# Even mixer in steps: the other projections one by one between a group's chunks

## Chip, cores and metric

The kernel runs on one core of a Trainium2 chip. The metric is the device time in microseconds (us) of one execution, as the median of several runs. The profile is one further execution, recorded by the hardware profiler. Engines are named as in the profile: PE does matmuls (PEld loads its weights), DVE is the vector engine, ACT the scalar engine, POOL is GpSimd (which issues the gathers here), SP issues the plain DMAs.

## What is computed

A two-layer backbone over 512 latent tokens ("x") and 256 context tokens ("c"), width 1024. Layer 0 is the even mixer followed by a PEER expert layer, layer 1 the odd mixer followed by another. Only layer 0 processes the context's outputs. The even mixer, cut to what matters here:

```
def even_mixer(hx, hc, w_in, w_out, ...):
    def project(h, conv):
        sc_x, sc_b, sc_c, z, xbc, dt_raw = jnp.split(h @ w_in, [...], axis=-1)
        xbc = jax.nn.silu(conv(xbc, ssd_conv_w) + ssd_conv_b)
        xs, bm, cm = jnp.split(xbc, [SSD_WIDTH, ...], axis=-1)
    ...                      # 16 heads in 4 groups, each a chunked scan in both directions
    def finish(gates, ssd_in, y_ssd, conv):
        y_a = sc_b * conv(sc_c * sc_x, sc_conv_w)              # short convolution
        y_b = (y_ssd + d_skip[:, None] * ssd_in[0]).reshape(Bsz, T, SSD_WIDTH)
        y_b = group_rmsnorm(y_b * jax.nn.silu(z), ssd_norm_w, SSD_GROUPS)
        return jnp.concatenate([y_a, y_b], axis=-1) @ w_out
```

The PEER layer picks 128 experts per token; for each it takes the dot product of the token with one row of a table U, puts it through a gelu and a gate, and adds so much of one row of a table V.

## The kernel before

A framework records instructions in program order, and its scheduler then sets a fixed order for each engine: what was recorded first goes first where several are ready. Each engine runs its list in order. Tiles come from pools with a number of buffers (`bufs`); a tile that finds no free buffer waits for an older one's last reader.

`even_mixer` runs twice, first for the context (T = 256, two chunks of 128 tokens), later for x (T = 512, `nt` = 4 chunks). For each half `q` it runs `ssd(g)` for two groups, then `short_conv(q)`, then `out_proj`, which multiplies the eight 128-row tiles of `yT` (four from the short convolution, j = 3 and 2, taken first; four from the groups, j = 1 and 0) with `w_out` and adds to the stream (L467, L471, L472). Within `ssd(g, yT)`:

- Four projections `proj` (24 matmuls each, L227) with weights that `weight` loads as two raw tiles `wr` of 512 KB, splits on ACT into `wh` (L197) and on DVE into `wl` (L198). ACT and DVE take each projection through the convolution into `ch` (L503, L354, L356); one Silu over `ch` (L506).
- For each chunk: transposes to `tk` (L513, L514), scaled inputs `xe` (L518), a state contribution `con` (L520, L521). Then the recurrence over chunks on DVE (`sd` L533, `con` L536).
- For each chunk: products `cb` (L551), exponents from `srow` and `trow` (L559 to L563 on PE, L565 on ACT), a multiplication `E` on DVE (L566), four matmuls into `yp` (L572).
- The gate `z`, two more projections (L577). The norm: L581, L583 on DVE, a square on ACT (L584), a sum over partitions on PE (L587, two matmuls), ACT and DVE to L595, and L598 writes `yT`.

`short_conv(q)` has twelve projections in six weights of two tiles: `scx` (L480), the products `scx` (L484), `sca` (L486, L354, L356), `yT` (L491).

While x's even mixer runs, the context's expert dot products (`dots`) run on the engines that it leaves free: they are recorded behind it, so the scheduler fills them in. There are 256: POOL issues an indirect gather of 128 rows of U (`g`, 512 KB, L950) into one of `gbufs` buffers, and DVE takes the dot product with the tokens (L1055). After the mixer come the PEER layer of layer 0 for x (first L109, L126) and the context's sums over rows of V.

```
for q in range(2):
    yT = P.tile([128, 8, T], F32, name="yT", tag="yT", bufs=1)
    for g in (2 * q, 2 * q + 1):
        ssd(g, yT)
    short_conv(q, yT)
    out_proj((D + q * 512, q * 512), yT)
```

Of the kernel before, what the change touches and what calls it, by code (L numbers as in the profile page):

```python
# [39 lines left out]
def kslab(ap, c0, n):  # L40

    return ap[:, c0:c0 + n].rearrange("(k p) n -> p k n", p=128)
# [21 lines left out]
class Backbone:  # L64
# [368 lines left out]
    def even_mixer(self, hT, T, width, steps, states, res, P, stream):  # L433
# [38 lines left out]
                    nc.vector.tensor_add(res[c][:, ns], res[c][:, ns], t)  # L472

        def short_conv(quarter, yT):
            for b in range(2 * quarter, 2 * quarter + 2):
                wx = self.weight([kslab(W, b * 256, 256)], KT, 256)
                sx, acc = [], []
                for e in range(2):
                    sx.append(P.tile([128, T], F32, name="scx", tag="scx", bufs=2))
                    nc.scalar.activation(sx[e], proj(wx, e), AF.Copy)  # L480
                wc = self.weight([kslab(W, 2048 + b * 256, 256)], KT, 256)
                for e in range(2):
                    j = 2 * b + e
                    nc.vector.tensor_mul(sx[e], proj(wc, e), sx[e])  # L484
                    acc.append(P.tile([128, T], F32, name="sca", tag="sca", bufs=2))
                    nc.scalar.activation(acc[e], sx[e], AF.Copy, scale=self.sc_w[:, j, 1:2])  # L486
                    self.conv(acc[e], sx[e], self.sc_w[:, j], rows, width)
                wb = self.weight([kslab(W, 1024 + b * 256, 256)], KT, 256)
                for e in range(2):
                    j = 2 * b + e  # L490
                    self.hook(nc.vector.tensor_mul(yT[:, 4 + j % 4], proj(wb, e), acc[e]))  # L491

        def ssd(g, yT):
            h0 = 4 * g
            ch = (P0 if T > 256 and g % 2 == 0 else P).tile([128, 4, T], F32, name="ch", tag="ch", bufs=nb)
            for j, t in enumerate((2 * g, 2 * g + 1, 8 + g, 12 + g)):
                if j == 0:
                    w = self.weight([kslab(W, 4096 + g * 256, 256)], KT, 256)
                if j == 2:
                    w = self.weight([kslab(W, 5120 + g * 128, 128), kslab(W, 5632 + g * 128, 128)], KT, 256)  # L500
                ps = proj(w, j % 2)
                acc = ch[:, j, :]
                nc.scalar.activation(acc, ps, AF.Identity, bias=self.ssd_b[:, t:t + 1],  # L503
                                     scale=self.ssd_w[:, t, 1:2])
                self.conv(acc, ps, self.ssd_w[:, t], rows, width)
            nc.scalar.activation(ch, ch, AF.Silu)  # L506

            tk = P.tile([128, nt, 3, 128], F32, name="tk", tag="tk", bufs=nb)
            con = P.tile([128, nt, 2, 256], F32, name="con", tag="con", bufs=nb)
            for c in range(nt):  # L510
                ps = self.tr_tile()
                for j in range(3):
                    nc.tensor.transpose(ps[:, j], ch[:, j, c * 128:(c + 1) * 128], self.ident)  # L513
                nc.scalar.activation(tk[:, c], ps[:, :3], AF.Copy)  # L514
                xt = tk[:, c, 0:2].rearrange("p a (b q) -> p (a b) q", q=64)
                xe = P.tile([128, 2, 4, 64], F32, name="xe", tag="xe", bufs=nb)
                for d in range(2):
                    nc.vector.tensor_mul(xe[:, d], xt, tend[:, c, d, h0:h0 + 4, None].to_broadcast([128, 4, 64]))  # L518
                ps = self.mc_tile()
                nc.tensor.matmul(ps, tk[:, c, 2], xe.rearrange("p a h q -> p (a h q)"), start=True, stop=True)  # L520
                nc.scalar.activation(con[:, c].rearrange("p a n -> p (a n)"), ps, AF.Copy)  # L521

            st = {}
            for d in range(2):
# [18 lines left out]
            for d in range(2):  # L543
                k = d * 16 + h0
                self.load(srow[32 * d:32 * d + 12], parts[:, 32 + k:36 + k])
                self.load(trow[32 * d + 12:32 * d + 15], parts[:, k:k + 4])
            for c in range(nt):
                cs = slice(c * 128, (c + 1) * 128)
                B, C = ch[:, 2, cs], ch[:, 3, cs]
                ps = self.mc_tile()  # L550
                nc.tensor.matmul(ps[:, :128], B, C, start=True, stop=True)  # L551
                cb = P.tile([128, 128], F32, name="cb", tag="cb", bufs=2)
                nc.scalar.activation(cb, ps[:, :128], AF.Copy)
                terms = [(0, cb), (1, cb)] + [(d, C) for d in range(2) if st[c, d] is not None]
                for i, (d, by) in enumerate(terms):
                    kr = slice(32 * d, 32 * d + 15)
                    ps = self.mc_tile().rearrange("p (h t) -> p h t", h=4)
                    if i < 2:
                        nc.tensor.matmul(ps, srow[kr, cs], trow[kr, :, cs], start=True, stop=False)  # L559
                        nc.tensor.matmul(ps, self.identb, self.mneg[:, d, None, :].to_broadcast([128, 4, 128]),  # L560
                                         start=False, stop=True)
                    else:
                        nc.tensor.matmul(ps, self.sel[kr], trow[kr, :, cs], start=True, stop=True)  # L563
                    e = P.tile([128, 4, 128], F32, name="E", tag="E", bufs=4)
                    nc.scalar.activation(e, ps, AF.Exp)  # L565
                    ins = nc.vector.tensor_mul(e, e, by[:, None, :].to_broadcast([128, 4, 128]))  # L566
                    if i == 0:
                        self.hook(ins)
                    for h in range(4):
                        p, x = h // 2, h % 2 * 64  # L570
                        l = tk[:, c, p, x:x + 64] if i < 2 else st[c, d][:, h * 64:h * 64 + 64]
                        nc.tensor.matmul(yp[p][x:x + 64, cs], l, e[:, h], start=(i == 0),  # L572
                                         stop=(i == len(terms) - 1), skip_group_check=True)
# [8 lines left out]
                                               op0=OP.mult, op1=OP.add)  # L582
            nc.vector.tensor_mul(y, y, zs)  # L583
            nc.scalar.activation(sq, y, AF.Square)  # L584
            ps = self.mc_tile()
            for p in range(2):
                nc.tensor.matmul(ps[:, :T], self.ones, sq[:, p], start=(p == 0), stop=(p == 1))  # L587
            r, hv = sq[:, 0], sq[:, 1]
            t = P.tile([128, T], F32, name="nt", tag="scx", bufs=2)
            nc.scalar.activation(t, ps[:, :T], AF.Ln, scale=1.0 / 256, bias=self.epsc)  # L590
            nc.vector.tensor_scalar(hv, ps[:, :T], -0.5 / 256, -0.5 * EPS, op0=OP.mult, op1=OP.add)
            nc.scalar.activation(r, t, AF.Exp, scale=-0.5)
# [3 lines left out]
            for p in (1, 0):  # L596
                k = 2 * g + p
                nc.vector.scalar_tensor_tensor(yT[:, k % 4], y[:, p], self.snw[:, k:k + 1], r,  # L598
                                               op0=OP.mult, op1=OP.mult)

        for q in range(2):
            yT = P.tile([128, 8, T], F32, name="yT", tag="yT", bufs=1)
            for g in (2 * q, 2 * q + 1):
                ssd(g, yT)
            short_conv(q, yT)
            out_proj((D + q * 512, q * 512), yT)
        return fin

# [805 lines left out]
    def build(self):  # L1414
        tc, nc, io = self.tc, self.nc, self.io
        with ExitStack() as es:
# [104 lines left out]
            with tc.tile_pool(name="evenhx", bufs=1) as H, Pools(tc, "evenx") as P:  # L1521
# [7 lines left out]
                ch.__exit__(None, None, None)  # L1529
                ch = right("ch2")  # L1530
                hp = ch.__enter__()
                self.gpool, self.gbufs = hp, 6
                todo = [lambda t=t, h=h: self.dots(0, t, h) for t in ctoks for h in range(8)]
                todo.insert(8 + TU, lambda: self.turn(ctoks[0]))
                self.between([], 1)
# [64 lines left out]
```

## Time and profile before

| | us |
|---|---|
| median of 3 runs (4576.45 to 4588.05) | 4577.45 |
| the profiled execution, own time | 4589.98 |
| its span, first to last instruction | 4587.9 |
| PE busy | 4200.4 (92%) |
| DVE busy | 3416.2 (74%) |
| ACT busy | 1761.5 (38%) |
| POOL busy | 1507.3 (33%) |

The span of this execution is taken apart by stretches. The context's mixer lies at about 45 to 335 us, x's mixer at about 460 to 1142 us. An engine's busy share is read within one stretch, since the stretches have different limits; granted clock 1.00 stands for 2.4 GHz on TensorE and 0.50 for 1.2 GHz.

### The profile page before, as it was taken

To read this page: it belongs to the slowest core of one execution; us is meant where nothing else is said; L and a number is where in the kernel's file an instruction comes from. 1 tells how busy PE (TensorE), PEld (TensorE's weight loads), DVE (VectorE), ACT (ScalarE), POOL (GpSimd) and SP (SyncE) were. 2 spreads that over 40 slices of the span, in tenths; PEclk is the share of its full clock that TensorE was granted. 3 is DMA by queue.
4 is the path that set the end of the run, shared out by engine and by line. 5 is a ranking of instruction groups with operands and counts; after the bars stand their busy time and mean duration, and the time that the engine had idled before them with its cause. 6 is when DMAs were issued, how large, how long until landed. Compare 5 with 4: busy or idle time off the path is not lost. (4 is left out here: it accounts for less than half of the span.)

```text
span 4587.9 us, 60287 instructions
## 1 busy us (share of the span) xinstructions
PE 4200.4 (92%) x21452; PEld 3359.2 (73%) x21452; DVE 3416.2 (74%) x6826; ACT 1761.5 (38%) x3159; POOL 1507.3 (33%) x1114
## 2 busy tenths in 40 slices
PE   7989947969988789999999999998999999999998
PEld 4666625635534778888899988886857778888997
DVE  4556989973686979888788865666887548878887
ACT  4442312231224833333333335554447433333333
POOL 0002477640444355544455410000000005445452
PEclk9999958969999999999999999998999999999999
DMA  9538889952777899988898831221246758889886
GB/s 322 175 105 280 276 310 339 346 182 89 254 244 257 270 333 354 365 319 314 316 329 322 324 123 57 62 60 49 74 156 189 231 183 315 321 314 335 326 315 224
DMA packets 488766, 1119.51 MB, mean 244 GB/s; under 512 B 39793, under 2 KB 252337, under 8 KB 488465
## 3 DMA queue, kind: packets, MB, share of 16 engines
q1 hardware_dynamic: 334096, 553.55, 36.2%
q0 software_dynamic: 154368, 562.11, 33.9%
q8 instruction: 169, 2.77, 0.2%
q14 instruction: 133, 1.08, 0.1%
HBM read 1054.18 MB, written 60.82 MB: 243 GB/s over the span
## 5 line engine op out<-in xcount | busy, mean ns | idle before, releaser
L950 POOL DMA_INDIRECT g<-in_peer_u_dram,idx x256 | 373.7, 1460 | 934.3 <-DVE pre L1055 699.0
L198 DVE TENSOR_TENSOR wl<-wr,wh 128x1024 fp32r<-128x1024 f32 x404 | 493.3, 1222 | 197.2 <-ACT wh L197 195.2
L227 PE MATMUL yp<-hTh,wh 128*128 128x384 f32 x1808 | 610.9, 338 | 13.5 <-ACT wh L197 12.3
L227 PE MATMUL yp<-hTh,wl 128*128 128x384 f32 x1808 | 611.8, 338 | 6.0 <-DVE wl L198 5.9
L197 ACT ACTIVATE wh<-wr 128x1024 fp32r<-128x1024 f32 x404 | 426.6, 1057 | 489.8 <-DMA wr<-in_peer_uT_dram 223.7
L227 PE MATMUL yp<-hTl,wh 128*128 128x384 f32 x1808 | 608.4, 336 | 0.0
L950 POOL DMA_INDIRECT g<-in_peer_v_dram,idx x256 | 386.0, 1508 | 381.5 <-DVE y L1075 311.1
L950 POOL DMA_INDIRECT g<-in_peer_v_dram,idxc x256 | 340.0, 1328 | 397.5 <-DVE y L1075 162.5
L950 POOL DMA_INDIRECT g<-in_peer_u_dram,idxc x256 | 346.4, 1353 | 156.3 <-DVE prec L1055 62.5
L86 POOL TENSOR_TENSOR rs_y<-rs_v,mhalf 128x1 f32<-128x1 f32 (+2 forms) x29 | 22.7, 783 | 1089.4 <-DVE rs_v L85 1089.3
L227 PE MATMUL mm<-hTh,wh 128*128 128x512 f32 (+1 forms) x864 | 342.9, 398 | 21.7 <-ACT scx L480 11.4
L227 PEld LDWEIGHTS yp<-hTh,wh 128*128 128x128 f32 x1808 | 341.9, 189 | 27.9 <-ACT wh L197 14.1
L198 DVE TENSOR_TENSOR vl<-wr,vh 128x1024 fp32r<-128x1024 f32 x256 | 312.6, 1221 | 63.8 <-ACT vh L197 63.5
L227 PEld LDWEIGHTS yp<-hTh,wl 128*128 128x128 f32 x1808 | 341.2, 189 | 12.9 <-DVE wl L198 11.1
L1055 DVE CUSTOM_DVE_ANT_0 g<-g,h 128x1024 f32<-128x1024 f32 x256 | 305.9, 1221 | 60.1 <-DMA g<-in_peer_u_dram,idx 59.8
L227 PEld LDWEIGHTS yp<-hTl,wh 128*128 128x128 f32 x1808 | 341.6, 189 | 9.0
L227 PE MATMUL mm<-hTl,wh 128*128 128x512 f32 (+1 forms) x864 | 339.6, 393 | 0.2 <-DVE hTl L198 0.2
L1351 DVE TENSOR_TENSOR a<-a,gt 128x384 f32<-128x384 f32 x256 | 215.6, 846 | 164.3 <-ACT a L1239 81.3
L1075 DVE SCALAR_TENSOR_TENSOR y<-g,pre,y 128x1024 f32<-128x1024 f32 x254 | 325.4, 1281 | 16.2 <-DMA g<-in_peer_v_dram,idx 14.9
L227 PE MATMUL mm<-hTh,wl 128*128 128x512 f32 (+1 forms) x864 | 335.3, 391 | 0.6 <-DVE wl L198 0.6
L1055 DVE CUSTOM_DVE_ANT_0 g<-g,cx 128x1024 f32<-128x1024 f32 x256 | 308.0, 1220 | 31.8 <-DMA g<-in_peer_u_dram,idxc 30.6
L197 ACT ACTIVATE vh<-wr 128x1024 fp32r<-128x1024 f32 x256 | 270.1, 1055 | 155.9 <-PE mc L1373 74.6
(462 smaller groups left out, 9685.6 us busy)
## 6 DMA issues: line engine op xcount, KB each, us to landing
wr<-in_peer_v_dram SPq DMA_DIRECT2D x256, 512.0 KB
wr<-in_peer_uT_dram SPq DMA_DIRECT2D x226, 512.0 KB
gd<-stage SPq DMA_DIRECT2D x24, 2048.0 KB
gt<-gd SPq DMA_DIRECT2D x64, 768.0 KB
wr<-in_ev_w_in_dram SPq DMA_DIRECT2D x80, 512.0 KB
adaw<-in_ada_w_dram SPq DMA_DIRECT2D x48, 512.0 KB
adaw<-in_ada_w_dram POOLq DMA_DIRECT2D x48, 512.0 KB, 6.6
wr<-in_peer_wq_dram SPq DMA_DIRECT2D x40, 512.0 KB
```

Of the source, the lines that this page charges most:

```text
L86: nc.gpsimd.tensor_tensor(y, v, self.mhalf[:, :n], op=OP.pow)
L197: self.nc.scalar.activation(hi, src, AF.Copy)
L198: self.nc.vector.tensor_sub(lo, src, hi.bitcast(F32))
L227: mm(o, a, rhs(kk, i)[b], start=first and kk == 0 and n == 0, stop=last and kk == k - 1 and n == 2)
L950: self.nc.gpsimd.indirect_dma_start(out=g, out_offset=None, in_=table, in_offset=bass.IndirectOffsetOnAxis(ap=idx, axis=0), element_offset ...
L1055: self.nc.vector.tensor_tensor_reduce(g, g, t.h2, 1.0, 0.0, OP.mult, OP.add, s["pre"][:, k, h:h + 1])
L1075: nc.vector.scalar_tensor_tensor(t.y, g, a, t.y, op0=OP.mult, op1=OP.add)
L1351: self.last = nc.vector.tensor_mul(a, a, self.gt_[:, :, i % 4])
```

## The change

`ssd` is taken apart: the four projections with their convolution become a generator `ssd_in(g)`, which stops after each projection; `short_conv` becomes a generator that stops after each of its twelve. A group's `ssd(g, yT, other)` gets one of them as `other`: for the first group of a half that is the second group's projections, for the second group the short convolution. It takes one step of `other` in the norm, in both streams; for x (T > 256) also after the contributions of the second and the fourth chunk and ahead of the third chunk's products. What is left of a generator runs where all of it ran before. To make room: `xe` has 2 buffers in x (it had 1; 2 KB each per partition), the norm's `nt` a buffer of its own (it shared `scx`), and the gathers `g` have 5 buffers, not 6, while x's mixer runs.

```diff
@@ short_conv: becomes a generator
                     nc.scalar.activation(sx[e], proj(wx, e), AF.Copy)
+                    yield
...
                     self.conv(acc[e], sx[e], self.sc_w[:, j], rows, width)
+                    yield
...
                     self.hook(nc.vector.tensor_mul(yT[:, 4 + j % 4], proj(wb, e), acc[e]))
-
-        def ssd(g, yT):
-            h0 = 4 * g
-            ch = (P0 if T > 256 and g % 2 == 0 else P).tile([128, 4, T], F32, name="ch", tag="ch", bufs=nb)
+                    yield
+
+        chs = {}
+
+        def ssd_in(g):
+
+            chs[g] = ch = (P0 if T > 256 and g % 2 == 0 else P).tile([128, 4, T], F32, name="ch", tag="ch", bufs=nb)
...
                 self.conv(acc, ps, self.ssd_w[:, t], rows, width)
+                yield
+
+        def ssd(g, yT, other):
+
+            h0 = 4 * g
+            ch = chs.pop(g)
...
-                xe = P.tile([128, 2, 4, 64], F32, name="xe", tag="xe", bufs=nb)
+                xe = P.tile([128, 2, 4, 64], F32, name="xe", tag="xe", bufs=2)
...
                 nc.scalar.activation(con[:, c].rearrange("p a n -> p (a n)"), ps, AF.Copy)
+                if T > 256 and c % 2:
+                    next(other, None)
...
             for c in range(nt):
+                if T > 256 and c == 2:
+                    next(other, None)
...
             nc.scalar.activation(sq, y, AF.Square)
+            next(other, None)
...
-            t = P.tile([128, T], F32, name="nt", tag="scx", bufs=2)
+            t = P.tile([128, T], F32, name="nt", tag="nt", bufs=1)
...
+        def rest(steps):
+            for _ in steps:
+                pass
+
         for q in range(2):
             yT = P.tile([128, 8, T], F32, name="yT", tag="yT", bufs=1)
-            for g in (2 * q, 2 * q + 1):
-                ssd(g, yT)
-            short_conv(q, yT)
+            first, second, short = ssd_in(2 * q), ssd_in(2 * q + 1), short_conv(q, yT)
+            for steps, g, other in ((first, 2 * q, second), (second, 2 * q + 1, short)):
+                rest(steps)
+                ssd(g, yT, other)
+            rest(short)
             out_proj((D + q * 512, q * 512), yT)
...
-                self.gpool, self.gbufs = hp, 6
+                self.gpool, self.gbufs = hp, 5
```

Since recorded order is priority, the scheduler's lists move by more than these lines. Three places. The line numbers of the changed kernel are higher there: its L525, L532, L588, L604, L608, L615 and L1078 are L513, L520, L572, L587, L591, L598 and L1055 of before.

First, PE in x's mixer from the norm of group 0 on (L587, L604), into the chunks of group 1. Before:

```order
L587 MATMUL mc_4638<-yT_4191,ones_80 128x512 x2
L513 MATMUL mc_4792<-ident_69,ch_4650 128x128 x3
L520 MATMUL mc_4800<-xe_4797,tk_4790 128x512
L513 MATMUL mc_4803<-ident_69,ch_4650 128x128 x3
L520 MATMUL mc_4811<-xe_4808,tk_4790 128x512
L513 MATMUL mc_4814<-ident_69,ch_4650 128x128 x3
```

and of after, where `mm_5460` is a projection of the short convolution:

```order
L604 MATMUL mc_4777<-yT_4191,ones_80 128x512 x2
L525 MATMUL mc_4792<-ident_69,ch_4356 128x128 x3
L227 MATMUL mm_5460<-hTh_2921,wl_5451 128x512
L227 MATMUL mm_5460<-hTh_2921,wh_5450 128x512
L227 MATMUL mm_5460<-hTl_2922,wh_5450 128x512
```

Before, no projection stands between the norms of groups 0 and 1; now the first L532 has 51 projection matmuls ahead of it, and 214 (8.9 projections) stand between the two norms.

Second, DVE at the norm of the last group, group 3, in x (L583, L591 and so on). Before:

```order
L583 TENSOR_TENSOR ch_6087<-ch_6087,yT_5628 128x1024
L591 TENSOR_SCALAR yT_5628<-mc_6533 128x512
L484 TENSOR_TENSOR scx_6557<-mm_6623,scx_6557 128x512
L593 TENSOR_TENSOR nt_6536<-yT_5628 128x512
L594 TENSOR_TENSOR nt_6536<-nt_6536,yT_5628 128x512
L354 SCALAR_TENSOR_TENSOR sca_6649<-scx_6557,sc_w_3450,sca_6649 128x8x63
```

and of after, where the first two rows are the last of the 256 dot products:

```order
L1078 ISA g_7837,prec1_2845<-g_7837,cx1_112 128x1024
L1078 ISA prec1_2845 128x1
L608 TENSOR_SCALAR yT_5628<-mc_6671 128x512
L610 TENSOR_TENSOR nt_6674<-yT_5628 128x512
L1085 TENSOR_TENSOR prec1_2845<-prec1_2845,gatec1_2844 128x128
L611 TENSOR_TENSOR nt_6674<-nt_6674,yT_5628 128x512
L612 SCALAR_TENSOR_TENSOR yT_5628<-nt_6674,yT_5628 128x512
L615 SCALAR_TENSOR_TENSOR yT_5628<-ch_5793,snw_3464,yT_5628 128x512 x2
L471 TENSOR_TENSOR ot_6995<-mc_6951,gate_6949 128x512
```

Before, the last dot product stands at the start of group 3's chunks and the short convolution's work behind the norm; now the chunks and the short convolution stand ahead of the last dot product, and only the norm and the sums of `out_proj` behind it.

Third, PE at the same norm. Before:

```order
L572 MATMUL yp_6292<-E_6458,fin_431 64x128 x2
L587 MATMUL mc_6533<-yT_5628,ones_80 128x512 x2
L227 MATMUL mm_6653<-hTh_2921,wh_6613 128x512
L227 MATMUL mm_6653<-hTl_2922,wh_6613 128x512
L227 MATMUL mm_6653<-hTh_2921,wl_6614 128x512
```

and of after:

```order
L588 MATMUL yp_6358<-E_6566,fin_431 64x128 x2
L467 MATMUL yp_6952<-wo_6955,yT_5628 128x512 x2
L467 MATMUL yp_6952<-wo_6965,yT_5628 128x512 x2
L467 MATMUL yp_6954<-wo_6955,yT_5628 128x512 x2
L467 MATMUL yp_6954<-wo_6965,yT_5628 128x512 x2
L604 MATMUL mc_6671<-yT_5628,ones_80 128x512 x2
L467 MATMUL mc_6951<-wo_6955,yT_5628 128x512 x2
```

Before, nine projections and then all 64 matmuls of `out_proj` stand behind the last norm; now eight of the 64 stand ahead of it and 56 behind, and no projection.

## Rows read from the trace of the kernel before

**Rows 1.** Busy time by stretch: us; busy us (instructions) by engine; clock; DMA share; GB/s

```profile
508.00:614.00 106.00, 74.54 (x381) 51.91 (x379) 99.22 (x172) 35.34 (x52) 77.31 (x55) 0.84 0.95 332
614.00:722.00 108.00, 48.75 (x202) 25.66 (x203) 96.73 (x172) 20.63 (x34) 86.69 (x64) 0.54 0.89 307
722.00:973.00 251.00, 218.07 (x872) 148.00 (x870) 234.53 (x383) 68.82 (x86) 175.61 (x133) 0.90 0.97 345
973.00:1034.00 61.00, 43.47 (x181) 20.64 (x181) 32.34 (x61) 19.93 (x34) 3.52 (x3) 0.53 0.13 43
1034.00:1142.00 108.00, 104.72 (x346) 64.87 (x346) 38.74 (x57) 17.34 (x22) 0.57 (x1) 1.00 0.29 90
...
508.00:982.00 474.00, 344.05 (x1458) 226.75 (x1456) 438.90 (x742) 127.17 (x175) 343.13 (x253) 0.80 0.94 332
```

**Rows 2.** Timelines: start us, us; DVE at the first and last dot, PE's last out_proj

```profile
508.91 1.23 DVE L1055 CUSTOM_DVE_ANT_0 g<-g,cx 128x1024 f32<-128x1024 f32 x1 [1.86 <-DMA g<-in_peer_u_dram,idxc]
...
983.46 0.08 DVE L1055 DVE_READ_ACCUMULATOR2_ANT prec<- 128x1 f32 x1
...
1138.17 1.88 PE L467 MATMUL yp<-wo,yT 128*128 128x512 f32 x4
```

**Rows 3.** Groups of instructions, 508 to 1150 us: xcount, busy us, mean ns, idle before

```profile
L1055 DVE CUSTOM_DVE_ANT_0 g<-g,cx 128x1024 f32<-128x1024 f32 x256 | 308.0, 1220 | 31.8 <-DMA g<-in_peer_u_dram,idxc 30.6
L198 DVE TENSOR_TENSOR wl<-wr,wh 128x1024 fp32r<-128x1024 f32 x41 | 50.0, 1221 | 13.3 <-ACT wh L197 13.3
L566 DVE TENSOR_TENSOR E<-E,cb 128x512 f32<-128x512 f32 x32 | 21.7, 685 | 11.0 <-ACT E L565 11.0
L1055 DVE DVE_READ_ACCUMULATOR2_ANT prec<- 128x1 f32 x256 | 20.4, 80 | 0.0
L518 DVE TENSOR_TENSOR xe<-tk,tend 128x256 f32<-128x256 f32 x32 | 12.2, 420 | 1.1 <-ACT tk L514 1.1
L354 DVE SCALAR_TENSOR_TENSOR sca<-scx,sc_w,sca 128x504 f32<-128x504 f32 x8 | 5.9, 743 | 1.6 <-ACT sca L486 1.6
L484 DVE TENSOR_TENSOR scx<-mm,scx 128x512 f32<-128x512 f32 x8 | 5.5, 688 | 5.8 <-PE mm L227 5.8
```

**Rows 4.** Timeline, DVE: the last norm in x

```profile
1027.20 1.16 DVE L583 TENSOR_TENSOR ch<-ch,yT 128x1024 f32<-128x1024 f32 x1
1034.04 0.69 DVE L591 TENSOR_SCALAR yT<-mc 128x512 f32<-128x512 f32 x1 [5.68 <-ACT nt L590]
1039.72 1.53 DVE L598 SCALAR_TENSOR_TENSOR yT<-ch,snw,yT 128x512 f32<-128x512 f32 x2
```

**Rows 5.** Timeline, PE: projection matmuls at full clock; out_proj, two records a matmul

```profile
1042.20 0.39 PE L227 MATMUL mm<-hTh,wh 128*128 128x512 f32 x1
1042.43 0.39 PE L227 MATMUL mm<-hTl,wh 128*128 128x512 f32 x1
...
1119.28 1.88 PE L467 MATMUL mc<-wo,yT 128*128 128x512 f32 x4
1121.00 1.88 PE L467 MATMUL yp<-wo,yT 128*128 128x512 f32 x4
```

**Rows 6.** POOL's gathers L950, 508 to 990 us: durations in ns, waits, landing

```profile
L950 POOL DMA_INDIRECT g<-in_peer_u_dram,idxc x253: 932/1427/1991, 508.2 to 976.1; - x127
...
  DVE prec L1055: 62.5, 61
  issue: 54.6, 179
...
DMA to landing us min/median/max: 5.2/6.4/10.4
```

**Rows 7.** Busy time by stretch, as rows 1: the highest DMA rate in x's mixer

```profile
760.00:780.00 20.00, 20.00 (x81) 16.31 (x80) 18.80 (x30) 4.12 (x5) 13.44 (x11) 0.90 1.04 392
```

**Rows 8.** Waits of PE, 45 to 360 us: us in total, times, longest

```profile
PE mc L587 <- ACT yT L584: 6.1, 3, 2.2
```

**Rows 9.** Busy time by stretch, as rows 1, in the context's mixer

```profile
60.00:130.00 70.00, 64.07 (x445) 41.96 (x444) 33.49 (x54) 34.16 (x51) 0.00 (x0) 1.00 0.96 328
```

## Prediction

> **What bounds the kernel now.** I read the busy time by stretch first, cutting x's mixer at the norms of its four groups (DVE's L591) [rows 1]. In the first three stretches, 508 to 973 us, DVE is busy 94%, 90% and 93% of the time, the DMA engines 95%, 89% and 97%, and PE only 70%, 45% and 87%, part of it at half clock (0.84, 0.54, 0.90). These stretches hold the context's dot products: the first starts at 508.9, the 256th ends at 983.5 [rows 2]. From there on DVE and DMA are nearly empty: 32 and 39 us of DVE in the last two stretches, DMA at 0.13 and 0.29, while PE is at work for 43 of 61 us at half clock (group 3's chunks) and for 105 of 108 us at full clock (nine projections and `out_proj`) [rows 1]. So x's mixer has two limits, one after the other: DVE, with DMA close by, until the last dot; PE from there to the last matmul at 1138.17 + 1.88 = 1140.05 [rows 2]. The wait that ends last is in the tail: 1140.05 - 983.5 = 156.5 us of PE and latency with nothing beside it. PE work that moves ahead of the last dot falls into PE's free time; its DVE work comes on top of a full DVE.
>
> **The change, part by part.** The sum is made in the profiled execution (span 4587.9, own time 4589.98); it stands 0.3% above the median, 4577.45, to which I apply the difference.
>
> *What the dots' stretch takes up.* By the order, DVE has this between the first and the last dot now: 256 dots of 1220 + 80 ns (333 us), 32 splits of 1221 (39), 48 `E` of 685 (33), 26 `xe` of 420 (11), 38 `sd` and `con` of the same size (16), 32 convolution halves of 743 (24), 24 products and sums of 688 (17), and some 20 us of norms and the first rows: 493 us [rows 3]. It takes 983.5 - 508.9 = 474.6 us, 0.963 of that, because records overlap a little and DVE waits a little. After the change these stand ahead of the last dot too: 16 `E` (11.0), 9 splits (11.0), 8 convolution halves (5.9), 8 products (5.5), 6 `xe` (2.5), 10 `sd` and `con` (4.2) and some 6 us of group 3's L581, L583, memsets and group 2's last norm steps: 46 us. Times 0.963 the last dot ends 44 us later, at 1027.5. The bound below is nothing: if DMA and not DVE set the pace, the 46 us fall partly into DVE's 7% of idle time (474 - 438.9 = 35 us [rows 1]), and the last dot comes 10 to 20 us later only.
>
> *What stays behind the last dot.* The five last dots stand between L583 and L591 and take 6.5 us; L583 to L591 takes 6.8 us anyway, for ACT's square and logarithm and the two matmuls of L587 [rows 4]. From L591 to the end of the first L598 it is 6.4 us (1034.04 to 1039.72 plus half of 1.53) [rows 4]. Eight matmuls of `out_proj` stand ahead of the norm and eight run under it; the other 48 need `yT`'s group tiles, at 1.72 us for two (four records) [rows 5]: 41.3 us. With 0.5 and 1 us for starting at half clock that is 49 us, in place of 156.5. So the end moves from 1140.05 to 1027.5 + 49 = 1076.5: **63 us gained**.
>
> *Does PE hold the pace?* The order gives, norm to norm, the work of each stretch at full clock: a projection is 24 x 0.227 = 5.45 us, a matmul of `out_proj` 0.86 [rows 5], and a group's chunks about 26 us (48.75 busy at clock 0.54, nothing else in the stretch [rows 1]). Group 0's stretch: 15.6 projections where 8.5 stood, 111 us of PE for 61 dots, 16 splits and a group's chunks, about 132 us of DVE. Group 1's: 8.9 projections and 8 of `out_proj` where none stood, 81 us of PE in 118. Group 2's: 16.9 projections and 56 of `out_proj`, 166 us of PE in 175 of DVE (84 dots, 16 splits). Group 3's: 33 in 93. Only group 2's is tight; before, the nearest case is 722 to 973, PE busy 218 of 251 us and DVE 235 [rows 1]. There neither engine can catch up on a wait of the other. I charge 10 us, between 0 (the stretch before ran at DVE's pace) and 30 (PE's 166 us at clock 0.81).
>
> *DMA.* Nine weight tiles move into the dots' stretch: 4.7 MB on top of 157, at 332 GB/s some 14 us of DMA beside 44 of DVE [rows 1]. It hides. In group 2's stretch 84 gathers, 16 weight tiles and `out_proj`'s 8 are 57 MB, 164 us at 345 GB/s [rows 1], nearly DVE's 175: this is inside the 10 us above. DMA ran at 392 GB/s in its best 20 us [rows 7], which would make it 144.
>
> *Five gather buffers.* A buffer is held from POOL's issue until its dot ends: 6.4 us to landing at the median, 10.4 at most [rows 6], 1.25 for the dot, 0.3 between issues (54.6 us over 179). With six buffers POOL could have a gather every 8 / 6 = 1.3 us, with five every 1.6; its own work is 343.13 / 253 + 0.3 = 1.66 [rows 1, 6]; the dots now come every (1027.5 - 508.9) / 256 = 2.0 us. POOL waits for free buffers already (62.5 us in 61 waits [rows 6]), and DVE waits 30.6 us for gathers [rows 3]. Runs of dots will find one buffer less filled ahead: I charge 4 us, between 0 and 20 (37 waits for gathers, half a microsecond longer each).
>
> *Queues and small things.* On SP the weight loads now stand ahead of some `srow` and `trow` loads and of `out_proj`'s weights; behind a load that waits for one of the two raw buffers these wait too, and group 1's norm on PE stands behind eight matmuls of `out_proj`. A load lands within some microseconds, DVE has dots meanwhile: 0 to 5 us, taken as part of the 10. Two `xe` buffers and a separate `nt` only remove waits of engines off the limit. ACT gets six table loads more and is at 38%.
>
> *Context.* PE is the limit there and waits 6.1 us for norms [rows 8]; a projection now stands in each norm. But from 60 to 130 us DMA is at 0.96 [rows 9], and the moved projections want their weights earlier. I take a gain of 2 us, between 8 gained and 4 lost.
>
> Sum: -63 + 10 + 4 - 2 = **-51 us**: 4577.45 - 51 = 4526. After x's mixer the order is nearly the same and PE the limit, so I let the difference stand in full.
>
> **Rivals.**
>
> 1. *DMA, not DVE, is the limit of the dots' stretch.* For it: 0.89 to 0.97 busy. Against: in the stretch with most weights and dots DVE never had more than 7% idle. Then the last dot is only some 14 to 20 us later and the gain is 75 to 95 us: about 4495.
>
> 2. *PE at half clock becomes the limit: slower.* Its place are the stretches of groups 1 and 2. Row 614 to 722 shows a granted clock of 0.54 with PE busy 45%, after waits of PE for DVE [rows 1]. If group 1's 81 us ran at 0.54, they would take 150 in place of 118; group 2's 166 at 0.75, 221 in place of 175. With 32 and 46 us lost and the tail's 63 gained, and 8 more as `out_proj` starts cold, that is +23: 4600. It decides from a clock of about 0.72 in group 2's stretch on (166 / 0.72 is 55 us over 175). Against it: 508 to 614 had PE busy 70% and a clock of 0.84, and both stretches will be at least that busy. The Trainium skill ("TensorE: Matmul & The Clock Gate", HAM oscillation — how this bites in real kernels) has the same mechanism: waits for data between short bursts put the clock back to half each time, and the projections now stand in short pieces between chunk matmuls that wait for DVE. No stretch here has that mix; by the page alone this rival would be the likely one.
>
> 3. *The gathers take over with five buffers.* If landing is near its longest, 10.4 us, a buffer is held for 12 and a dot comes every 2.4 us: 612 us for 256, some 93 later than forecast, +40. From about 9.6 us to landing on, nothing is gained. More likely is part of it: no change, about 4575. Against: the median, 6.4, in stretches with DMA at 0.95.
>
> 4. *The change moves less than it says.* The scheduler had overlapped group 1's projections with group 0's chunks already (8.5 of them), so only half of what the code moves is new. The order speaks against it where it counts, at the tail; if waits there give half back, 4550.
>
> **How the numbers follow.** Forecast with its bounds (4505 to 4560): 0.70. Rival 1: 0.10. Rival 2: 0.06. Rival 3: 0.08. Rival 4: 0.06. About 0.3% (14 us) is what a measurement of this kernel can tell from no change. Faster by more than that (below 4563.7): the forecast, rival 1, rival 4 and a little of rival 3, 0.86; within: most of rival 3 and the forecast's upper end, 0.08; slower: rival 2, 0.06. The range takes in rival 1's nearer part and rival 4: 4496 to 4562.
>
> **What would show it.** Right: the last dot product near 1025 to 1040; DVE above 90% busy up to it; after it a tail of about 50 us with only `out_proj` on PE; granted clock above 0.7 in group 1's stretch and 0.85 in group 2's; the context's mixer within 8 us. Wrong: PE fully busy at a low clock around 640 to 930 with DVE waiting for PE (rival 2); DVE's waits for gathers far above 31 us in all (rival 3); the last dot before 1010 (rival 1); a tail of more than 70 us (rival 4); or a different PEER layer behind the mixer, which the sum leaves out.

## The result, and the profile after

The changed kernel takes **4513.23 us** (median of 4 runs, 4502.13 to 4516.54); beside it the kernel before took 4582.74 (4 runs, 4576.45 to 4588.05). The ratio is **0.9846**, 95% interval 0.9825 to 0.9867: 69 us, or 1.5%, faster. The forecast was 4526, between 4496 and 4562. The profiled execution of after has a span of 4509.7 us and an own time of 4511.87. Its busy times by engine, which answer to the table of before:

```profile
PE 4184.6 (93%) x21452; PEld 3343.7 (74%) x21452; DVE 3413.7 (76%) x6826; ACT 1766.2 (39%) x3165; POOL 1499.5 (33%) x1114
```

No engine has less to do than before by more than 16 us (PE, 4200.4 before), and the span is 78 us shorter: most of what is gone is time in which engines stood. In the changed kernel L525, L532, L588, L604, L608, L615, L973 and L1078 are L513, L520, L572, L587, L591, L598, L950 and L1055 of before.

Busy time by stretch of after, cut at the norms of the four groups as [rows 1] (us; busy us and instructions of PE, PEld, DVE, ACT, POOL; granted clock; DMA share; GB/s):

```profile
502.00:628.00 126.00, 113.20 (x557) 83.80 (x556) 121.03 (x202) 52.64 (x70) 81.49 (x62) 0.93 0.95 335
628.00:743.00 115.00, 95.81 (x421) 62.27 (x420) 109.85 (x186) 37.67 (x52) 76.66 (x60) 0.88 0.90 307
743.00:920.00 177.00, 164.64 (x693) 108.12 (x692) 163.86 (x270) 51.19 (x70) 107.09 (x85) 0.96 0.94 332
920.00:1013.00 93.00, 53.56 (x208) 25.58 (x207) 86.21 (x153) 22.88 (x38) 66.22 (x48) 0.60 0.85 291
1013.00:1061.00 48.00, 45.75 (x107) 19.57 (x105) 17.00 (x34) 2.39 (x4) 0.57 (x1) 1.00 0.26 82
```

DVE is now busy for 121, 110, 164 and 86 us of the first four stretches, 93 to 96% of each (90 to 94% in the three that held the dots before). What has changed is the last row: 48 us, where 156.5 us lay behind the last dot. Timelines of DVE and PE (start and duration, us), which answer to [rows 2] and [rows 4]:

```profile
502.58 1.23 DVE L1078 CUSTOM_DVE_ANT_0 g<-g,cx 128x1024 f32<-128x1024 f32 x1 [1.92 <-DMA g<-in_peer_u_dram,idxc]
...
1004.46 1.22 DVE L599 TENSOR_TENSOR ch<-ch,yT 128x1024 f32<-128x1024 f32 x1
...
1013.20 0.08 DVE L1078 DVE_READ_ACCUMULATOR2_ANT prec<- 128x1 f32 x1
1013.20 0.69 DVE L608 TENSOR_SCALAR yT<-mc 128x512 f32<-128x512 f32 x1
...
1057.48 1.88 PE L467 MATMUL yp<-wo,yT 128*128 128x512 f32 x4
```

The last dot ends at 1013.3 with the last norm's first step right behind it, and x's mixer ends at 1059.4. Set against before, the end of x's mixer moves by -80.7 us: -6.3 up to the first dot (508.9 to 502.6), +36.1 between first and last dot (474.6 to 510.7), -110.4 behind it (156.5 to 46.1). Of that 2.5 us are given back later; the spans differ by 78.2.

### The profile page after: what moved, and what is told of

It reads as the page before. It is cut to its first block, busy times and chain, and to the rows that moved or that the text cites. A ratio compares the mean times of both kernels' runs of the same rounds, so it can differ in the third digit from the quotient of the medians.

```text
span 4509.7 us, 60276 instructions
## 1 busy us (share of the span) xinstructions
PE 4184.6 (93%) x21452; PEld 3343.7 (74%) x21452; DVE 3413.7 (76%) x6826; ACT 1766.2 (39%) x3165; POOL 1499.5 (33%) x1114
## 5 line engine op out<-in xcount | busy, mean ns | idle before, releaser
L973 POOL DMA_INDIRECT g<-in_peer_u_dram,idx x256 | 373.8, 1460 | 934.7 <-DVE pre L1078 691.1
L973 POOL DMA_INDIRECT g<-in_peer_v_dram,idx x256 | 387.6, 1514 | 380.1 <-DVE y L1098 313.9
L973 POOL DMA_INDIRECT g<-in_peer_v_dram,idxc x256 | 341.3, 1333 | 399.7 <-DVE y L1098 167.2
L973 POOL DMA_INDIRECT g<-in_peer_u_dram,idxc x256 | 334.9, 1308 | 204.6 <-DVE prec L1078 125.3
L1078 DVE CUSTOM_DVE_ANT_0 g<-g,h 128x1024 f32<-128x1024 f32 x256 | 305.4, 1218 | 61.6 <-DMA g<-in_peer_u_dram,idx 60.9
L1396 PE MATMUL mm<-vh,ah 128*128 128x512 f32 x768 | 304.3, 396 | 29.2 <-ACT vh L197 20.2
L197 ACT ACTIVATE ah<-a 128x384 fp32r<-128x384 f32 x256 | 133.7, 522 | 503.5 <-DVE a L1374 407.6
```

Of the source, the lines that this page charges most:

```text
L197: self.nc.scalar.activation(hi, src, AF.Copy)
L973: self.nc.gpsimd.indirect_dma_start(out=g, out_offset=None, in_=table, in_offset=bass.IndirectOffsetOnAxis(ap=idx, axis=0), element_offset ...
L1078: self.nc.vector.tensor_tensor_reduce(g, g, t.h2, 1.0, 0.0, OP.mult, OP.add, s["pre"][:, k, h:h + 1])
L1396: ins = nc.tensor.matmul(acc[t][hlf], x[:, ts], y[:, hlf * 512:(hlf + 1) * 512], start=(i == 0 and n == 0), stop=(i == 127 and n == 2))
```

## Experiments

Twelve kernels were run. The table has each one's device time (median, or the time of a single run), its ratio to the kernel before where that was timed beside it, and the profiled execution's first dot, last dot and end of x's mixer (the last `out_proj` matmul), read from the timelines as above. Runs of the same kernel lie up to 35 us apart (before, 4566 to 4601), so a single run can't show a difference of 10 us; the stretches of a trace show where time went in that one execution.

| kernel | us | ratio (95%) | first dot | last dot | end of x's mixer | span |
|---|---|---|---|---|---|---|
| before | 4582.74 | 1 | 508.9 | 983.5 | 1140.1 | 4587.9 |
| after | 4513.23 | 0.9846 (0.9825 to 0.9867) | 502.6 | 1013.3 | 1059.4 | 4509.7 |
| ctx_only | 4514.88 | 0.9845 (0.9814 to 0.9877) | 503.0 | 1023.1 | 1069.3 | 4512.5 |
| x_only | 4501.66 | 0.9817 (0.9782 to 0.9853) | 505.2 | 1015.0 | 1061.1 | 4501.2 |
| norms | 4525.69 | single run | 504.4 | 1025.2 | 1072.7 | 4523.9 |
| x_chunks | 4511.23 | single run | 499.4 | 1017.3 | 1062.6 | 4509.1 |
| before_5bufs | 4584.85 | 1.0009 (0.9991 to 1.0027) | 509.0 | 1004.1 | 1133.7 | 4572.7 |
| nt_only | 4522.23 | 0.9868 (0.9846 to 0.9889) | 504.1 | 1023.0 | 1069.6 | 4521.7 |
| after_scx | 4557.5 | 0.9945 (0.9925 to 0.9965) | 513.6 | 1018.1 | 1114.1 | 4562.5 |
| half_dots | 4400.31 | single run | 502.2 | 1039.0 | 961.2 | 4398.5 |
| more_dve | 4552.06 | single run | 502.2 | 1218.1 | 1068.0 | 4550.3 |
| after_4bufs | 4520.11 | single run | 502.0 | 1085.6 | 1048.0 | 4518.4 |
| after_3bufs | 4506.13 | single run | 501.9 | 1287.7 | 1046.2 | 4504.4 |
| early_out | 4501.31 | 0.9837 (0.981 to 0.9863) | 500.3 | 1011.6 | 1058.1 | 4499.2 |

### Which part of the change carries the gain?

**ctx_only**: steps in the context's norms alone; x's generators run whole, where they ran before. The buffers stay as in after.

```diff
-                if T > 256 and c % 2:
-                    next(other, None)
...
-                if T > 256 and c == 2:
-                    next(other, None)
...
-            next(other, None)
+            if T <= 256:
+                next(other, None)
```

> The changed kernel with the steps taken in the context's norms only; in x no step is taken, so its projections are recorded as before, but with the new buffers (two xe, own nt, five gather buffers). Theory (the order in x carries the gain): the first dot stays at about 502 us as in the changed kernel, the dots' stretch is back at about 475 us, the tail from the last dot to the last out_proj matmul back at about 156 us; time about 6 us under before, no change that can be measured. Rival (the room made for buffers carries it): the tail stays under 100 us and the time under 4540.

Measured 4514.88, ratio 0.9845 against after's 0.9846: the gain is there with not one step in x. The theory that the recorded order of x's steps carries it fell. The time goes where it goes in after; three of the rows of ctx_only, the stretches of groups 2 and 3 and the tail:

```profile
748.00:914.00 166.00, 155.98 (x664) 102.84 (x663) 156.07 (x258) 50.32 (x69) 105.78 (x83) 0.97 0.94 332
914.00:1018.00 104.00, 65.20 (x244) 33.24 (x242) 94.04 (x163) 25.26 (x40) 70.64 (x52) 0.62 0.88 296
1018.00:1069.00 51.00, 42.94 (x98) 19.02 (x98) 16.53 (x33) 1.46 (x3) 0.57 (x1) 0.93 0.25 81
```

**x_only**: the other half, steps in x alone, none in the context's norms.

```diff
-            next(other, None)
+            if T > 256:
+                next(other, None)
             ps = self.mc_tile()
```

> The changed kernel without the step in the context's norms. Theory: the context's steps are worth 6 us and nothing in x hangs on them: first dot at about 509 us, dots' stretch about 511, tail about 46, time 6 us over the changed kernel, some 64 us under before. Rival (the earlier start comes from elsewhere): the first dot stays at 502 to 504.

Measured 4501.66, ratio 0.9817, not slower than after. Its first dot starts at 505.2, 2.6 us later than after's, and nothing of that shows in the time. The forecast of 509 was missed: 3.7 of the 6.3 us by which the dots start earlier than before are there without the context's steps. So neither half of the steps is needed. **norms** (a step in each norm, none between x's chunks) and **x_chunks** (steps between x's chunks, none in a norm) were run once each:

```diff
# norms
-                if T > 256 and c % 2:
-                    next(other, None)
...
-                if T > 256 and c == 2:
-                    next(other, None)
# x_chunks
-            next(other, None)
             ps = self.mc_tile()
```

> The changed kernel with the steps in the norms alone, none between the chunks of x. One of four steps is left in each group. Theory (the steps between the chunks place the work ahead of the last dot): the tail is 90 to 130 us and the dots' stretch 480 to 495, the sum some 25 us under before. Rival (one step in the norm is enough for the scheduler to fill the rest): tail under 60 us.

> The changed kernel with the steps between x's chunks but none in any norm. Theory (three of four steps in x are left, and the scheduler fills in the rest): first dot at about 509 us, stretch 500 to 512, tail 46 to 60, end of out_proj at 1065 to 1085. Rival (the step in the norm is the one that fills the idle time): tail above 80.

4525.69 and 4511.23 us: any selection of steps gives most of the gain. Both missed their forecasts. The tail behind the last dot is 47.5 us in norms, where the theory said 90 to 130. In x_chunks, which has no step in the context either, the first dot comes at 499.4, the earliest of all, where 509 was forecast; so the steps in the context's norms are not what lets the dots start earlier. What all these kernels share is not a step but the room made: five gather buffers, two `xe`, an `nt` of its own. The first of these was taken alone. **before_5bufs**:

```diff
-                self.gpool, self.gbufs = hp, 6
+                self.gpool, self.gbufs = hp, 5
```

> The kernel before with five gather buffers in place of six and nothing else. Theory (POOL has slack, DVE sets the pace): the dots' stretch grows by 0 to 4 us from 474.6, time as before within 0.3%. Rival (gathers limited by buffers, the 4 us I charged and up to 20): stretch 485 to 495, time 10 to 20 us over before.

Ratio 1.0009, interval 0.9991 to 1.0027: in the time, one gather buffer less costs nothing and gains nothing. Its dots' stretch did grow, from 474.6 to 495.1 us, which is what the rival forecast; but x's mixer ends no later for it (1133.7 against 1140.1), since PE's work behind the last norm still follows. In its scheduler's lists PE's order has the same counts of projections between the norms as before.

The trace of before had held the answer, in rows that the prediction did not read. ACT there from 714 us on, behind the norm of group 1 (start, us; what it waited for), and the short convolution's first evacuations L480 from 600 to 760 us (times waited for, who waited):

```profile
715.91 0.69 ACT L590 ACTIVATE nt<-mc,epsc 128x512 f32<-128x512 f32 x1 [2.57 <-PE mc L587]
716.49 0.59 ACT L480 ACTIVATE scx<-mm 128x512 f32<-128x512 f32 x1
...
736.28 0.60 ACT L480 ACTIVATE scx<-mm 128x512 f32<-128x512 f32 x1 [9.96 <-DVE yT L595]
```

```profile
L480 ACT ACTIVATE scx<-mm x4: 580/590/597, 716.5 to 758.2; 128x512 f32<-128x512 f32 x4
...
  DVE yT L595: 10.0, 1
who waited for it (us, times):
  PEld mm L227: 12.6, 3
  PE mm L227: 10.2, 3
```

L480 copies a projection from PSUM; it reads nothing that L595 writes. Yet it waits for L595, the last reader of group 1's `nt`. The two share the tag `scx` with two buffers, and the recorded order puts groups 0's and 1's `nt` ahead of the first `scx`. So the first copy goes out right behind L590, which begins group 1's `nt`, and the second when L595 has let go of it. Until then the projections' results stay in PSUM, and the projections behind them stand too. It is the place in the order that does it, not the number of buffers: with a third buffer for the tag the scheduler's lists keep the same counts of projections from norm to norm (lists alone; this was not run). No projection ran between the norms of groups 0 and 1.

**nt_only** is before with five gather buffers (without which the tile has no room) and this one line, and no step anywhere; **after_scx** is after with the line undone.

```diff
# nt_only, against before_5bufs; after_scx undoes this line in after
-            t = P.tile([128, T], F32, name="nt", tag="scx", bufs=2)
+            t = P.tile([128, T], F32, name="nt", tag="nt", bufs=1)
```

> Before with five gather buffers and the norm's tile in a buffer of its own; no steps, one xe buffer. Theory: the shared tile held the short convolution back. It comes from a place in the recorded order: group 1's nt stands ahead of the short convolution's first two scx, with two buffers for all of them, so that ACT may not empty the short convolution's projections before group 1's norm is through. With a tile of its own the gain is there without steps: 17 projections ahead of group 0's norm, none behind group 3's, x's mixer 75 to 85 us shorter, 4510 to 4520 us. Rival: the second xe buffer carries it, or both are needed: 4575 to 4590.

> After, with the norm's tile back among the short convolution's (steps, two xe buffers and five gather buffers kept). Theory: the steps are a second way to the same end, and a lesser one: they record six of each half's twelve short projections ahead of the group's norm, so six of the nine projections leave the tail, 6 x 5.45 = 33 us, and three with the 64 matmuls of out_proj stay behind the last norm, some 75 us from it to the end; x's mixer 55 to 60 us shorter than before, about 4535 us (4520 to 4550). Rival: the steps carry nothing at all without the tile: 4575 to 4590. Rival: they carry everything: 4513.

nt_only: 4522.23, ratio 0.9868, 58.8 us under the kernel before beside it; that is 2 us above its forecast of 4510 to 4520, and x's mixer ends 70 us earlier where 75 to 85 were forecast. after_scx: 4557.5, ratio 0.9945, 23.5 us under it. **One line without steps brings 59 us, the steps (with the second `xe` buffer) without the line 24, all together 70.** The numbers of projections that the scheduler's lists put on PE ahead of each norm of x, counted from the first dot on, show why (with the matmuls of `out_proj`, 64 a half, in brackets):

| | to norm 0 | to norm 1 | to norm 2 | to norm 3 | behind |
|---|---|---|---|---|---|
| before | 8.5 | 0 | 24 (64) | 0 | 9 (64) |
| after_scx | 6.5 | 8 | 16 (64) | 8 | 3 (64) |
| nt_only, ctx_only | 17.3 | 7.2 (8) | 15.6 (56) | 1.4 (8) | 0 (56) |
| after | 15.6 | 8.9 (8) | 16.9 (56) | 0.1 (8) | 0 (56) |

L480's waits in nt_only, and PE's first waits in the stretch of group 1 in before (614 to 722 us) and in nt_only (635 to 748 us; total us, times, longest):

```profile
L480 ACT ACTIVATE scx<-mm x8: 579/598/601, 556.4 to 897.2; 128x512 f32<-128x512 f32 x8
...
  PE mm L227: 6.0, 4
who waited for it (us, times):
```

```profile
PE mc L520 <- DVE xe L518: 26.9, 4, 8.0
PE yp L572 <- DVE con L536: 15.7, 1, 15.7
PE mc L587 <- ACT yT L584: 12.3, 1, 12.3
```

```profile
PE mc L520 <- DVE xe L518: 10.2, 2, 5.4
PE yp L572 <- DVE E L566: 6.2, 4, 3.4
PE yp L467 <- DVE ch L581: 5.1, 1, 5.1
```

The first `scx` is copied at 556.4 in place of 716.5, it waits for its own projection alone, and nobody waits for it. The projections that then run ahead fill the waits of PE in group 1's chunks.

after_scx missed its forecast of 4520 to 4550 by 7.5 us. Its tail is what was expected: 1039.4 to 1114.1 is 74.8 us (75 forecast). What did not come is an earlier last norm: 1039.4, where before has 1034.0. Its L480, here L481, still waits for norms twice (L612, the last reader of `nt`), and twice for the convolution that reads an older `scx`:

```profile
  DVE yT L612: 9.3, 2
  DVE sca L356: 8.8, 2
```

and in the stretch of group 2, which still holds all 64 matmuls of `out_proj`, DVE is busy 198 of 225 us and PE 184. Which wait there ends last was not followed further.

Whether x's steps bring anything on top of the line is only half settled. The three kernels with steps between x's chunks (after, x_only, x_chunks) end x's mixer at 1059.4, 1061.1 and 1062.6; the three without them (ctx_only, norms, nt_only) at 1069.3, 1072.7 and 1069.6. That is 9.5 us by the means and the groups don't overlap. The intervals of after's and nt_only's ratios do, and ctx_only, which is after without the steps in x, has after's ratio. The second `xe` buffer was not run alone; nt_only shows that it isn't needed. By the scheduler's lists it moves no projection by itself, and the steps without it give the counts of after_scx; neither was run.

### What sets the pace while the dots run?

**half_dots**: after, with the context's dot products over the first 512 of 1024 columns only (the gathers bring whole rows as ever). **more_dve**: after, with one more DVE operation of 128x256 behind each dot, whose result is not used.

```diff
# half_dots
-            self.nc.vector.tensor_tensor_reduce(g, g, t.h2, 1.0, 0.0, OP.mult, OP.add, s["pre"][:, k, h:h + 1])
+            n = 512 if t.stream == "c" else D
+            self.nc.vector.tensor_tensor_reduce(g[:, :n], g[:, :n], t.h2[:, :n], 1.0, 0.0, OP.mult, OP.add, s["pre"][:, k, h:h + 1])
# more_dve, behind the unchanged line
+            if t.stream == "c":
+                self.nc.vector.tensor_mul(g[:, :256], g[:, :256], t.h2[:, :256])
```

> The changed kernel with the context's dot products taken over half of each gathered row; the gathers and all else stay whole (the other half of the products is left out). That takes about 0.55 us off each of 256 dots, some 140 us of DVE. Theory (DVE first, then DMA, PE and POOL close behind): the dots' stretch falls from 511 to 430 to 470 us, where DMA (some 162 MB at 345 GB/s is 470, at 392 GB/s 413), PE (427 busy) and POOL (256 times 1.61) are next; the tail stays at about 46. Rival (DMA is the limit): stretch stays above 495.

> The changed kernel with one more DVE instruction (128x256 products into the gather's own buffer, results unused) behind each of the 256 dots: 256 times about 0.42 us, 0.34 from start to start. Theory (DVE sets the pace of the dots' stretch): 511 us grow by 85 to 105 us. Rival (DMA or POOL set it): by less than 50, since DVE then has idle time to give.

half_dots: 4400.31 us, x's mixer over at 961.2, 98 us earlier than after's. The forecast, a dots' stretch of 430 to 470 us with a tail of 46, missed the form: 24 dots now come behind the mixer, the last at 1039.0, so that the stretch from first to last dot is 537 us. The mixer is therefore measured to its last norm, which starts at 906.3, 404 us behind the first dot; in after it is 511. From there to the end of the mixer it takes 55 us. The stretches of groups 1 to 3, and from the first dot to the last norm:

```profile
591.00:683.00 92.00, 92.00 (x463) 64.90 (x462) 78.16 (x169) 36.29 (x54) 50.52 (x47) 1.00 0.95 333
683.00:827.00 144.00, 144.00 (x612) 92.46 (x611) 105.83 (x238) 54.28 (x70) 79.75 (x74) 1.00 0.95 342
827.00:906.00 79.00, 76.75 (x388) 51.21 (x387) 64.27 (x143) 29.03 (x45) 41.87 (x40) 0.98 0.95 335
502.00:906.00 404.00, 393.89 (x1866) 264.18 (x1865) 315.99 (x702) 157.76 (x221) 221.88 (x204) 0.98 0.95 336
```

With DVE relieved (316 busy of 404 us), PE is busy 394 of 404 at clock 0.98 and is the limit. By itself this run doesn't rule out DMA as the limit in after: 204 gathers go out up to the last norm in place of 253, so DMA too has less to move. more_dve does. The same stretch, first dot to last norm, in after and in more_dve:

```profile
502.00:1013.00 511.00, 427.21 (x1873) 279.76 (x1872) 480.95 (x808) 164.38 (x228) 331.46 (x253) 0.87 0.92 320
502.00:1009.00 507.00, 429.08 (x1869) 281.80 (x1868) 466.22 (x862) 160.62 (x224) 245.68 (x189) 0.87 0.78 254
```

In more_dve still fewer gathers (189) stand beside the mixer and DMA falls to 0.78, yet the stretch takes 507 us, with DVE busy for 466 of them. The stretch follows DVE's work and not DMA's. So in after DVE sets the pace of x's mixer, and PE is the next limit, some 107 us behind.

more_dve: 4552.06 in a single run, some 39 us above after's median for 106.1 us of added DVE work (256 operations, 421 ns in the mean, by its trace). The forecast of a stretch longer by 85 to 105 us was wrong in form: x's mixer ends only 8.6 us later, and the last dot comes at 1218.1, 150 us behind its end. The scheduler lets the dots, which are recorded behind the mixer, fall back into the PEER layer.

### Do fewer gather buffers cost?

```diff
# after_4bufs; after_3bufs has 3
-                self.gpool, self.gbufs = hp, 5
+                self.gpool, self.gbufs = hp, 4
```

> The changed kernel with four gather buffers in place of five. A buffer is held about 6.3 + 1.25 + 0.3 us, so four give a dot every 1.96 us at best, 502 us for 256; the stretch takes 511. Theory (buffers at the edge): the stretch grows by 5 to 25 us. Rival (gathers land faster when fewer are in flight): by under 5 us.

> The changed kernel with three gather buffers. At a hold of 7.85 us a dot every 2.6 us, 670 us for 256: the stretch grows by about 160 us, or by about 20 if gathers land in the shortest time seen, 4.7 us. Theory: clearly slower, 50 to 160 us more. Rival (holding time isn't what counts): under 20 us.

4520.11 and 4506.13 us in a single run each, against a range of 4502 to 4517 for after. The dots' stretch grew even more than forecast (583.6 and 785.7 us, from 510.7), but three buffers do not cost the 50 to 160 us that were expected, which was the price in rival 3, and for four no cost can be told from the spread. What happens instead is seen in POOL's gathers (count, what POOL waited for, landing) of after, 502 to 1015 us, and of after_3bufs, 502 to 990:

```profile
L973 POOL DMA_INDIRECT g<-in_peer_u_dram,idxc x253: 932/1183/1987, 501.8 to 1005.6; - x127
...
  DVE prec L1078: 125.3, 113
...
DMA to landing us min/median/max: 4.7/6.3/9.8
```

```profile
L973 POOL DMA_INDIRECT g<-in_peer_u_dram,idxc x181: 933/1145/1987, 503.4 to 988.2; - x181
...
  DVE prec L1078: 256.3, 156
...
DMA to landing us min/median/max: 4.1/5.4/8.8
```

With three buffers POOL waits 256 us for a free one and 181 gathers, not 253, go out beside the mixer. The mixer ends 13 us earlier (at 1046.2), with fewer dots for DVE to take in it. DVE is busy for 398 us of the 488 up to the last norm and waits 80 of the rest for gathers (26 in after), so its list still sets the pace. The last dots run until 1287.7, beside the PEER layer of x. From the mixer's end on the kernel then takes 3458 us, against 3450 in after (3439 to 3452 in the kernels whose dots end with the mixer). Work was moved, not added. With four buffers this is less clean: the mixer ends 11 us earlier, but the rest takes 3470 us, 20 longer than in after, in that one execution; why is open.

### A last half in another order

**early_out**: after, with the last half's `out_proj` cut by rows of `yT`: both column halves of j = 3 and 2 first, so that 32 of the 64 matmuls need no group tile.

```diff
+        def last_out(rows, yT):
+            pss = [[self.mm_tile() for _ in range(3)] + [self.yp_tile()],
+                   [self.yp_tile()] + [self.mc_tile() for _ in range(3)]]
+            for js in ((3, 2), (1, 0)):
+                for n in range(2):
...
-            out_proj((D + q * 512, q * 512), yT)
+            (last_out if T > 256 and q else out_proj)((D + q * 512, q * 512), yT)
```

> The changed kernel with x's last out_proj in another order: the short convolution's part (j = 3 and 2) of both halves of the columns first, the first half's sums in three of the PSUM tiles that the projections no longer need; 18 of 64 matmuls stand ahead of the last norm in place of 8. Theory (PE alone sets the tail behind the last norm): ten matmuls of 0.86 us less behind it, the tail falls from 46 to 37 to 40 us and the time by 6 to 9 us against the changed kernel. Rival (the weights' loads wait for their two buffers and now come last): tail 44 us or more, no gain.

4501.31 us, ratio 0.9837 (0.981 to 0.9863). From the last norm to the end of x's mixer it takes 41.0 us (1017.0 to 1058.1), 5 less than after, between the theory (37 to 40) and the rival (44 or more). PE waits 2.1 us for a load of `out_proj`'s weights there, which is a part of the rival. The time cannot be told from after's by the intervals, which overlap.

## Why the prediction was right, and where it was not

**The bound and the place** were right. DVE took 42 us more in the dots' stretch (480.95 busy of 511 in after, 438.90 of 474 in [rows 1]), forecast from 46 us of durations; the stretch grew by 36.1 us, where the first term said 44, as DVE's idle time fell from 35 to 30 us. So one sign of being right was missed: the last dot came at 1013.3, not at 1025 to 1040 (6.3 us by the earlier start, 8 by the shorter stretch). half_dots and more_dve together show DVE as the limit and PE behind it.

**The tail** was right: 46.1 us, where the sum had 49. The microsecond in it for a start at half clock is not seen: the granted clock from 1013 us on is 1.00.

**The charges** for PE's tightness (10) and for five gather buffers (4) were not needed. Group 2's stretch, for which 175 us and 10 were reckoned, took 177 at clock 0.96; before_5bufs and the kernels with four and three buffers show no cost in the time that can be told from the spread. These 14 us and the 8 by which the first term was too high are most of what the forecast fell short by in the profiled executions (51 forecast, 78.2 between the spans); in the medians, where before lies 7 us lower than its profiled execution, it was 69.5.

**The context** came out as a size inside the bounds (-6.3 in the trace, -2 forecast, 8 gained to 4 lost), with the wrong reason. nt_only has no step there and its first dot comes at 504.1; after_scx has the step and starts at 513.6. In the context, too, the shared tile decides: the 6.1 us of PE's waits for norms [rows 8] are gone in nt_only, and 4.0 remain in after_scx.

**The step that failed** is the one sentence: "Two `xe` buffers and a separate `nt` only remove waits of engines off the limit." It costed at nothing the term that brings 59 of the 70 us, and gave the steps the whole. ACT is indeed not the limit, but its list is in order and its copies empty the PSUM tiles that PE's projections need; a wait of an engine at 38% stood on the path of the one that sets the tail. The total was right all the same, since it was worked out from where the instructions stand, norm to norm, in the two orders, whatever put them there. For the same reason the sentence that the buffers were "to make room" was no more than a description, and the count of 8.5, 0, 24, 0, 9 projections, quite uneven, was a question that the prediction did not ask.

**The rivals.** DMA as the limit: no, though the 78 us between the spans lie in this rival's 75 to 95; with DMA at 0.78 the mixer of more_dve is no shorter. PE at half clock as the limit: no; the granted clock was 0.88 and 0.96 in the stretches named, where the decision lay at about 0.72. Within group 1's stretch of after the clock does fall behind waits of PE: to 0.72 from 670 to 680 us and to 0.50, which is 1.2 GHz, from 710 to 720, each time after 10 us in which PE was busy 44% and 53%. The prediction had cited the Trainium skill ("TensorE: Matmul & The Clock Gate", HAM oscillation — how this bites in real kernels) for a clock that falls behind waits between short bursts; the trace agrees that it falls, but the stretch took 115 us, where 118 were reckoned for DVE. Rival 3's arithmetic of buffers held is seen in POOL's waits, which rose from 62.5 us [rows 6] to 125.3, but not its price: the end of x's mixer does not wait for the dots, and with three buffers they finish 241 us behind it without loss. Rival 4, that the change moves less than it says: true of the steps, which alone bring 24 us, not of the change.

## What to carry to other kernels

When an engine waits for an instruction whose result it does not read, look for the tile that the two share: a short-lived tile under another's tag can hold back a whole row of work that is recorded later. Before reordering by hand, ask why the scheduler left the gap; here one buffer of 2 KB per partition gave 59 of 70 us, and the reordering without it 24. And cost the pieces of a change apart, the ones "to make room" too: a total read from the order can be right while its cause is not.

## What the runs showed of the hardware that was not expected

- With three gather buffers in place of five the median landing time fell from 6.3 to 5.4 us, the longest from 9.8 to 8.8, and the 256 dots took 786 us in place of 511; in the one run no cost in the time shows.
- In group 1's stretch, where projections stand in short runs between chunk matmuls that wait for DVE, the granted clock is 0.88 (after) and 0.79 (nt_only), against 0.54 in the same stretch of before; in group 3's, with PE busy 54 to 65 us of 93 to 106, it stays near half speed (0.60 and 0.65).
